# The steps of the reciprocal root: mean and intermediate value kept in PSUM beside the sums

## The chip, the cores and the metric

The kernel runs on one core of one Trainium2 chip. The metric is the device time in microseconds (us) of one execution. The median of the runs before the change is the reference point.

## The reference

Two transformer layers work on 512 tokens and 256 context tokens, both 1024 wide, in float32. In layer 0 the mixer joins a gated chunk MLP and a differential attention; in layer 1 it is a windowed attention with a sink. Each layer ends in a gated feed-forward block. What matters here is the norm that stands ahead of every block, on the attention output of each head of layer 0, and at the end:

```
def rmsnorm(x, g):
    xf = x.astype(jnp.float32)
    y = xf * lax.rsqrt(jnp.mean(xf * xf, axis=-1, keepdims=True) + EPS)
    return (y * g.astype(jnp.float32)).astype(x.dtype)
```

## The kernel before, in words

Activations lie transposed: 128 features on the partitions, tokens along the free dimension. A norm therefore needs a sum across partitions and, once the root is known, a spreading of one number per token over all partitions. Both go through TensorE.

`rstd_diag` (L145) does the first half. For each block of 128 tokens, L156 (and L161 for squares that were not added up beforehand) multiplies the squares with a matrix of ones. The result is one PSUM bank in which row p, column 128*j of a tile `ps` holds the sum of token 128*j+p; all 128 columns of a block hold the same number. VectorE (DVE) reads one column per block and turns it into mean plus epsilon: L164 in general, L166 for the heads of layer 0. That goes to a small SBUF tile `sm` of 128 x nb elements, nb being 2, 3, 4 or 6. `rsqrt_small` (L131) computes the reciprocal root from it: a first guess with integer arithmetic on the bits (L135), then three steps of three instructions each (L137, L138, L139) on SBUF tiles, ten instructions in a chain in which each needs the one before. L173 then multiplies the identity with each root, which gives nb diagonal 128 x 128 blocks, and `spread` (L183) multiplies these with ones on TensorE, which leaves the root of each token on all partitions in PSUM.

There are fourteen such chains, in order of time: the first norm of the tokens, that of the context, four heads of layer 0 (each with two sum tiles, 4 and 2 blocks), the two halves ahead of each feed-forward block (two and two), the two norms between layer 0 and layer 1, and the two halves of the final norm. A fifteenth use of `rsqrt_small`, in the chunk MLP (`rstd_small`, L125), has its input in SBUF.

The banks come from tags. `bank()` gives one of three PSUM banks (`pb` in the profile), `fill()` the only bank of its tag (`pf`), `single()` one of four (a `pw`). A bank is given out again when every instruction on its tile has ended. The heads of layer 0 take `pb` banks for their sums and for the attention itself: in `attend` (L556 on) L564 transposes exponentials into a `pb` tile, ACT and DVE split it into two SBUF tiles (L122, L123), matmuls (L106 to L108) add it into another `pb` tile, which L576 copies out.

The order of each engine's instructions is set when the program is built: a list scheduler with a model of the times takes, for each engine, the ready instruction that stands first in the program, with a few constraints written by hand (`issue_after`, `high_priority`). GpSimd (POOL) makes the low halves of the split weights (L84, L879) and some sums of squares (L791). In the last stage (`final`, L1468) it multiplies some of the output tiles (L1475), and DVE does the others (L1477).

## Time and profile before

| | |
|---|---|
| median of 3 runs | 1608.77 us (1605.66 to 1609.75) |
| the profiled execution's own time | 1603.73 us |
| its span, first to last instruction | 1601.9 us |
| mean granted TensorE clock | 0.986 |
| busy: PE / DVE / ACT / POOL | 1524.8 / 1076.4 / 722.9 / 846.9 us |

The profile is of one execution. Starts in it are microseconds from the first instruction. PE is the matmul side of TensorE, PEld its weight load. In the rows of the time-ordered view the first column is the start, the second the time to the end of the merged group, then engine, line, operation, output and inputs by the program's names, shape, and count; in brackets stands the idle time of the engine just before and what ended it.

### The profile page before, as it was taken

The numbers are of one execution on the slowest core, as the hardware profiler recorded it, in microseconds if no ns is written. First come the engines' busy times: TensorE is split into PE (matmuls) and PEld (weight loads), VectorE is DVE, ScalarE is ACT, GpSimd is POOL, SyncE is SP. The second block draws the span as 40 slices with busy tenths as digits, with TensorE's granted clock in tenths as the row PEclk, the third lists the DMA queues.
The fourth block names the chain that finished last, engine by engine and source line by source line (L and its number), as shares of the span: only waits on it lengthen the run. The fifth ranks groups of instructions, "written<-read, shape, count | busy, mean of one in ns | idle before, by whom it ended". The sixth has DMA issues, their size and how long they took to land.

```text
span 1601.9 us, 24950 instructions
## 1 busy us (share of the span) xinstructions
PE 1524.8 (95%) x9547; PEld 1354.8 (85%) x9547; DVE 1076.4 (67%) x1949; ACT 722.9 (45%) x1472; POOL 846.9 (53%) x574
## 2 busy tenths in 40 slices
PE   6999988999999999999999989999999899999996
PEld 4776877889988898999999978777869799999996
DVE  3720788765687888777676486665667966666656
ACT  2412676553542323332333244556655644444442
POOL 0463211061265767766776415541304688888883
PEclk9999999999999999999999999999999999999998
DMA  8845100033133334434442022110225133323301
GB/s 325 305 145 184 40 8 1 24 121 119 66 95 109 125 119 139 137 122 149 141 137 85 27 65 66 60 34 9 72 80 204 53 102 101 115 86 113 93 14 53
DMA packets 54295, 162.00 MB, mean 101 GB/s; under 512 B 6176, under 2 KB 10656, under 8 KB 46496
## 3 DMA queue, kind: packets, MB, share of 16 engines
q1 hardware_dynamic: 47120, 135.11, 25.3%
q10 hardware_dynamic: 7056, 25.30, 4.9%
q8 instruction: 75, 1.23, 0.3%
q14 instruction: 44, 0.36, 0.1%
HBM read 158.29 MB, written 2.10 MB: 100 GB/s over the span
## 4 chain that ended last, share of the span: by engine, by line
PE 79%; DVE 13%; ACT 3%; issue 3%; DMA 1%; POOL 0%; SPq 0%; POOLq 0%; DVEq 0%; ACTq 0%
PE pw L106 11%; PE pw L107 11%; PE pw L108 10%; PE pb L107 8%; PE pb L106 8%; PE pb L108 8%; PE pf L106 4%; PE pf L107 4%; PE pf L108 4%; DVE junk L228 3%; PE pb L1408 2%; PE pb L1397 2%; PE pf L359 2%; PE pw L1360 1%; DMA ar<-ada 1%
## 5 line engine op out<-in xcount | busy, mean ns | idle before, releaser
L84 POOL TENSOR_TENSOR w<-raw,w 128x512 fp32r<-128x512 f32 (+1 forms) x84 | 128.0, 1530 | 241.9 <-ACT w L81 219.2
L106 PE MATMUL pw<-ax,w 128*128 128x384 f32 (+2 forms) x732 | 233.9, 323 | 4.4 <-ACT ax L200 1.6
L107 PE MATMUL pw<-ax,w 128*128 128x384 f32 (+2 forms) x732 | 234.7, 321 | 2.0 <-DVE ax L466 1.4
L108 PE MATMUL pw<-ax,w 128*128 128x384 f32 (+2 forms) x732 | 233.7, 320 | 1.4 <-DVE w L944 1.4
L774 DVE SCALAR_TENSOR_TENSOR xT<-pb,mod,xT 128x512 f32<-128x512 f32 (+3 forms) x208 | 145.8, 706 | 118.2 <-PE pb L108 118.0
L879 POOL TENSOR_TENSOR w<-raw,w 128x512 fp32r<-128x512 f32 x114 | 179.6, 1590 | 39.6 <-ACT w L879 39.4
L879 POOL TENSOR_TENSOR w<-t,w 128x512 fp32r<-128x512 f32 x102 | 157.1, 1544 | 60.9 <-ACT w L879 60.9
L106 PE MATMUL pb<-hh,w 128*128 128x512 f32 x480 | 172.5, 359 | 7.8 <-DVE xT L774 5.2
L107 PE MATMUL pb<-hh,w 128*128 128x512 f32 x480 | 172.4, 359 | 3.5 <-POOL hh L123 2.8
L108 PE MATMUL pb<-hh,w 128*128 128x512 f32 x480 | 172.2, 359 | 0.0
L107 PE MATMUL pw<-T,w 128*128 128x384 f32 (+1 forms) x508 | 157.1, 310 | 1.2 <-DVE T L123 1.2
L108 PE MATMUL pw<-T,w 128*128 128x384 f32 (+1 forms) x508 | 157.1, 310 | 0.0
L106 PE MATMUL pw<-T,w 128*128 128x384 f32 (+1 forms) x508 | 156.4, 310 | 0.0
L106 PEld LDWEIGHTS pw<-ax,w 128*128 128x128 f32 x732 | 139.1, 191 | 12.9 <-ACT ax L200 2.4
L107 PEld LDWEIGHTS pw<-ax,w 128*128 128x128 f32 x732 | 139.4, 191 | 10.2 <-DVE ax L466 3.1
L106 PE MATMUL pf<-ax,w 128*128 128x256 f32 (+2 forms) x420 | 139.9, 333 | 8.3 <-DVE qf L252 5.5
L108 PEld LDWEIGHTS pw<-ax,w 128*128 128x128 f32 x732 | 139.4, 191 | 4.1 <-DVE w L944 1.7
L108 PE MATMUL pf<-ax,w 128*128 128x256 f32 (+2 forms) x420 | 138.8, 330 | 0.0
L107 PE MATMUL pf<-ax,w 128*128 128x256 f32 (+2 forms) x420 | 138.8, 330 | 0.0
L228 DVE SCALAR_TENSOR_TENSOR junk<-ar,cb 128x1024 bf16<-128x1024 f32 x64 | 111.1, 1735 | 8.7 <-DMA ar<-ada 8.1
L879 POOL TENSOR_TENSOR w<-rawo,w 128x512 fp32r<-128x512 f32 x60 | 108.9, 1816 | 11.9 <-ACT w L879 11.9
L879 DVE TENSOR_TENSOR hs<-hs,pw 128x384 f32<-128x384 f32 (+1 forms) x114 | 55.2, 484 | 87.3 <-PE pw L108 74.8
(377 smaller groups left out, 3938.0 us busy)
## 6 DMA issues: line engine op xcount, KB each, us to landing
raw<-ffn_in SPq DMA_DIRECT2D x44, 1024.0 KB, 5.0
ar<-ada SPq DMA_DIRECT2D x24, 1024.0 KB, 7.0
ar<-ada ACTq DMA_DIRECT2D x48, 512.0 KB, 3.5
rawo<-ffn_out SPq DMA_DIRECT2D x88, 256.0 KB, 3.0
raw<-odd_out SPq DMA_DIRECT2D x32, 256.0 KB, 2.7
raw<-qk SPq DMA_DIRECT2D x16, 256.0 KB, 7.8
raw<-uv SPq DMA_DIRECT2D x16, 256.0 KB, 2.7
raw<-even_out SPq DMA_DIRECT2D x8, 512.0 KB, 3.5
```

The costliest lines, as they stand in the source:

```text
L84: eng.tensor_tensor(lo, raw, hi.bitcast(F32), ALU.subtract)
L106: mm(out, s[0], m[0], start=start, stop=False, **kw)
L107: mm(out, s[0], m[1], start=False, stop=False, **kw)
L108: return mm(out, s[1], m[0], start=False, stop=stop, **kw)
L228: return self.nc.vector.scalar_tensor_tensor(junk, t, 1.0, self.cb[who], ALU.mult, ALU.mult, accum_out=self.acc[who][:, col:col + 1])
L359: nc.tensor.matmul(ps[32 * q:32 * q + 32, :w], cst[:, k, :], t[:, w * q:w * q + w], start=k == 0, stop=k == KT - 1, skip_group_check=True)
L774: ins = self.nc.vector.scalar_tensor_tensor(h, ps[:, r], self.modcol(l, j, m, who), h, ALU.mult, ALU.add)
L879: tail[key] = fn(*args, **kw)
L1360: nc.tensor.matmul(ps[:, st:en], Q, K[g][p][:, b0 * P:b1 * P], start=p == 0, stop=p == 1, skip_group_check=True)
L1397: last = nc.tensor.transpose(pt[:, x * P:(x + 1) * P], es[2 * (x % 2) + x // 2][:, kb * P:(kb + 1) * P], self.ident)
L1408: nc.tensor.matmul(po[64 * h:64 * h + 64, :], V[vb][:, 64 * g:64 * g + 64], t[:, h * TC:h * TC + TC], start=kb == 0, stop=kb == nb - 1, sk ...
```

## The change

A new function `rsqrt_room` takes the mean `v` and a place `t` for the intermediate value from outside. `rstd_diag` passes both as columns of the first sum tile: columns 1 to nb for the mean, columns 33 to 32+nb for the intermediate value. Column 0 of each block still holds the sum that is read, and the other columns of the bank held copies that nobody reads. Only the root `y` is a small SBUF tile, as before. The products are grouped differently, so that each instruction takes one operand from PSUM and one from SBUF: before, y times y times v; now, v times y times y. The number of instructions is the same. `rsqrt_small` stays for the chunk MLP.

```
+    def rsqrt_room(self, v, n, t):
+
+        ve = self.nc.vector
+        y = self.small(n)
+        ve.tensor_scalar(y.bitcast(I32), v.bitcast(I32), -0.5, float(0x5F3759DF), ALU.mult, ALU.add)
+        for _ in range(3):
+            ve.tensor_tensor(t, v, y, ALU.mult)
+            ve.scalar_tensor_tensor(t, t, -0.5, y, ALU.mult, ALU.mult)
+            ve.scalar_tensor_tensor(y, t, 1.5, y, ALU.add, ALU.mult)
+        return y
...
-        ms = self.small(nb)
+        ms, room = None, None
...
             col = ps[:, 0:T].rearrange("p (j f) -> p j f", f=P)[:, :, 0]
+            if ms is None:
+                ms, room = ps[:, 1:1 + nb], ps[:, 33:33 + nb]
...
-        r = self.rsqrt_small(ms, nb)
+        r = self.rsqrt_room(ms, nb, room)
```

## The prediction

> **What bounds the kernel now.** I read the busy times first, then the chain of work that ended last, then the fourteen chains by a table over stretches, then the time order where one of them is stretched.

> ```profile
> PE 1524.8 (95%) x9547; PEld 1354.8 (85%) x9547; DVE 1076.4 (67%) x1949; ACT 722.9 (45%) x1472; POOL 846.9 (53%) x574
> ```

> ```profile
> PE 79%; DVE 13%; ACT 3%; issue 3%; DMA 1%; POOL 0%; SPq 0%; POOLq 0%; DVEq 0%; ACTq 0%
> ```

> PE bounds the whole; DVE (VectorE) holds 13% of the chain that ended last. A change on DVE counts only in those places. The next table takes, for some stretches that each hold one chain without its diagonal, the small tiles alone: the stretch, its length, DVE's busy time on them, and the count.

> ```profile
> 14.00:16.24 2.24, 1.80 (x11) 0.00 (x0) 1.00 1.03 410
> 45.70:54.24 8.54, 4.82 (x11) 0.00 (x0) 1.00 1.03 419
> 226.20:238.51 12.31, 1.91 (x12) 0.00 (x0) 0.86 0.00 0
> 268.60:279.46 10.86, 1.83 (x12) 0.00 (x0) 1.00 0.01 2
> 411.50:414.90 3.40, 2.99 (x11) 0.00 (x0) 1.00 0.55 188
> 1234.50:1237.25 2.75, 2.40 (x10) 0.00 (x0) 1.00 0.70 221
> 1583.70:1587.31 3.61, 2.32 (x11) 0.00 (x0) 1.00 0.02 5
> ```

> Undisturbed, eleven instructions take 1.80 us of a stretch of 2.24: 0.164 us each, one every 0.20. The second row is 3.02 above that, the last three 1.19, 0.76 (ten instructions) and 0.52 us. The two heads (12 instructions each) are not stretched, only drawn out by other work between the steps. What stretches a step shows between the layers:

> ```profile
> 949.73 2.61 POOL L84 TENSOR_TENSOR w<-raw,w 128x512 fp32r<-128x512 f32 x2 [4.04 <-ACT w L81]
> ```

> ```profile
> 949.89 1.23 DVE L137 TENSOR_TENSOR sm<-sm 128x2 f32<-128x2 f32 x1
> 951.05 0.74 DVE L199 SCALAR_TENSOR_TENSOR t<-xT,mod,pf 128x512 f32<-128x512 f32 x1
> 951.71 0.65 DVE L138 SCALAR_TENSOR_TENSOR sm<-sm,sm 128x2 f32<-128x2 f32 x1
> 952.28 0.74 DVE L201 SCALAR_TENSOR_TENSOR ax<-t,mod,ax 128x512 fp32r<-128x512 f32 x1
> ```

> POOL (GpSimd) works from 949.73 to 952.34, two instructions of 1.3 us. L137, both inputs in SBUF, takes 1.23 us and ends with the first of them; L138 takes 0.65 and ends with the second. L199, which reads PSUM and one SBUF tensor, runs beside the second from 951.05 in 0.74 us, no longer than L201 takes after POOL has ended. So the stall belongs to two SBUF inputs beside a working POOL, and the change takes it from all nine steps of a chain. The biggest case is the last chain:

> ```profile
> 1589.04 4.12 POOL L1475 TENSOR_TENSOR xT<-xT,rs 128x256 f32<-128x256 f32 x6 [3.68 <-ACT rs L1465]
> 1589.79 0.68 DVE L138 SCALAR_TENSOR_TENSOR sm<-sm,sm 128x2 f32<-128x2 f32 x1
> ...
> 1593.22 0.48 DVE L173 TENSOR_SCALAR dg<-ident,sm 128x128 f32<-128x128 f32 x2
> ...
> 1593.76 1.22 PE L183 MATMUL pf<-dg,ones 128*128 128x256 f32 x2 [5.20 <-DVE dg L173]
> 1595.07 0.37 ACT L1465 COPY rs<-pf 128x256 f32<-128x256 f32 x1 [6.10 <-PE pf L183]
> ...
> 1595.52 2.09 POOL L1475 TENSOR_TENSOR xT<-xT,rs 128x256 f32<-128x256 f32 x3 [2.35 <-ACT rs L1465]
> ```

> PE idles 5.20 us for this diagonal, ACT 6.10 for PE, POOL 2.35 for ACT. Nothing covers the chain; it is the end of the kernel.

> **The change part by part.** *The last chain.* Its last five steps lie from 1589.79 to 1593.22, 3.43 us. At one every 0.20 they take 1.0, and the diagonal could start 2.4 us earlier, at 1590.8. But there POOL is still at its six multiplications (until 1593.16), and the diagonal, with input and output in SBUF, can wait for POOL too:

> ```profile
> 944.42 1.26 POOL L84 TENSOR_TENSOR w<-raw,w 128x512 fp32r<-128x512 f32 x1 [6.73 <-ACT w L81]
> 944.48 1.88 DVE L173 TENSOR_SCALAR q<-ident,sm 128x128 f32<-128x128 f32 x4
> ```

> Four diagonals took 1.88 us there, where twice 0.48 would do. At the end each of the two diagonals can be held until an instruction of POOL ends (4.12/6 = 0.69 us each, half of it on the mean), which gives back up to 0.9 in all. Gain 1.5 to 2.4; I take 1.9, the middle. The chain before it loses its 0.52 too, but PE's sums for the last chain don't come earlier by that; what little it brings is inside the 1.9.

> *Between the layers.* L137 and L138 lose 1.23 + 0.65 - 2 x 0.16 = 1.56 us. But L201 has two SBUF inputs and would now arrive at about 951.1, just as POOL's second instruction has started: it would wait to 952.34, run 0.74, and end near 953.0, as it does now. The stall only changes its instruction. Bounds 0 and 1.56; I take 0.3, nearer to what the rows give.

> *The covered chains* (3.02, 1.19, 0.76). What PE waits for in them:

> ```profile
> PE pw L107 <- DVE ax L466: 1.4, 2, 0.8
> ```

> ```profile
>   PE pf L183: 6.6, 2
> ...
>   PE pb L183: 1.3, 2
> ```

> The first row is of the waits from 40 to 62: PE waited 1.4 us for products that DVE had queued around the second row's chain. The other two list who waited for the small tiles' chains in the whole run: PE's spreading four times, 5.20 of the 6.6 in the last chain. So at 411 and 1234 the diagonal was there before PE came to it, and 1.19 and 0.76 are worth nothing as long as PE's order has dense matmuls ahead of L183; without that cover they would count as they stand. Around 46 to 54 the bounds are 0 and 1.4; I take 0, since the small chain is only a part of what lay ahead of those products.

> *Each instruction by itself.* PSUM as an input is in the trace; PSUM as DVE's output is not.

> ```profile
> L138 DVE SCALAR_TENSOR_TENSOR sm<-sm,sm x42: 147/161/1245, 14.7 to 1591.9; 128x2 f32<-128x2 f32 x18, 128x6 f32<-128x6 f32 x12, 128x4 f32<-128x4 f32 x6, 128x3 f32<-128x3 f32 x6
> ...
> L166 DVE SCALAR_TENSOR_TENSOR sm<-pb,sx x8: 124/156/161, 226.3 to 319.8; 128x4 f32<-128x4 f32 x4, 128x2 f32<-128x2 f32 x4
> ```

> Minimum, median and maximum in ns: 156 with a PSUM input, 161 without. A PSUM input costs nothing. For the output I take the same, the nearest row; the spread of L166 (124 to 161) bounds it at about 0.04 us either way. It counts in four chains, the last two and the two between the layers: 44 instructions, 1.8 us either way. [...]

> *The bank.* This is the wait that the change adds. The first sum tile stays in use until the chain's last step. In `pf` and `pw` nobody wants the bank before the spreading. For the heads it is one of three `pb`, now free after one read at the start of the two long stretches of the table, then held for all of their 12.31 and 10.86 us if DVE's order stays. In them lie:

> ```profile
> 232.58 1.05 PE L564 MATMUL pb<-ident,e 128*128 128x128 f32 x4
> ...
> 233.00 0.68 DVE L123 TENSOR_TENSOR atl<-pb,ath 128x512 fp32r<-128x512 f32 x1
> ```

> ```profile
> 272.83 0.60 PE L564 MATMUL pb<-ident,e 128*128 128x128 f32 x4
> ...
> 274.12 0.68 DVE L123 TENSOR_TENSOR atl<-pb,ath 128x512 fp32r<-128x512 f32 x1
> ```

> One of the other two banks is the attention's sum, so the second block's transposes (L564) must wait until DVE has split the first (L123), to 233.68 and 274.80: 1.1 and 2.0 us. Behind them on PE stand the next scores, and for those wait DVE's maxima and ACT's exponentials.

> ```profile
> 226.00:281.00 55.00, 44.32 (x257) 37.71 (x256) 46.43 (x135) 38.14 (x75) 7.43 (x5) 0.91 0.00 1
> ```

> In these 55 us PE is busy for 44.32 and DVE for 46.43, so with 8.6 idle on the fullest engine most of 3.1 can be caught up. Bounds 0 and 3.1; I take 0.8, a quarter. The third head's chain is short, and the fourth has no attention behind it.

> **Sum** against the profiled execution: -1.9 - 0.3 + 0 + 0.8 = -1.4 us, from 1603.73 to 1602.3 (its span is 1601.9, and the 1.8 around it don't change). The profiled execution lies 5.0 us under the median of the runs; the forecast for the median is 1608.77 - 1.4 = 1607.4 us.

> **The rivals.** *The bank serializes the attention* (slower). If the steps stay as far apart as now, each further block of transposes in the hold has to wait for the split of the one before: transposes 0.60, DVE 0.68 and ACT's part, some 2 us. With two late blocks at each of two heads that is 8 us, less 1.9 at the end: +6, or 1615. It decides itself at whether the chain still runs when the second block is due; today it does, by 5.9 and 6.6 us. Against it: PE has other work ready, and nothing but the interleaving keeps a chain from its 2.24 us.

> *All stalls come back* (faster). If the covered 3.02 and the 1.56 lie on the path as well, the gain is 1.9 + 3.0 + 1.6 - 0.8 = 5.7: 1603.1. For it: DVE is in the chain in both places. Against it: the waits of only 1.4 us and the collision at 951.1.

> *Writing PSUM is slower*: at 0.04 us for 44 instructions the sum is +0.4, 1609.2.

> *The stalls stay*, because the one SBUF input that is left meets POOL as well: the change doesn't do what it can, and the bank's 0.8 remains, 1609.6. Against it stands L199 at 951.05.

> **How the numbers follow.** The forecast has 0.48, with a range of its own from -5 to +2; the bank 0.22; all stalls back 0.14; slower writes 0.09; stalls that stay 0.07. About 0.3% (4.8 us) is what a measurement of this kernel tells from no change. Faster by more: nearly all of "all stalls back" and a small part of the forecast, 0.17. Slower: the bank near its price, and the tails of the others where the scheduler's order shifts, 0.20. Within: 0.63. For 8 in 10 the range reaches from "all stalls back" with 2 us more to the bank's price: 1601 to 1615.

> **What would show it.** Right: no step above 0.2 us beside a working POOL; PE's idle time ahead of the last L183 down from 5.20 to about 3.3; L201 stalled near 951. The bank: a longer time from 226 to 281, with PE idle ahead of L564. Wrong: steps above 0.2 us without POOL beside them (slow PSUM writes), steps of 0.65 beside L1475 (stalls that stay), or another order of the heads that moves more than all these terms.

## The result and the profile after

The changed kernel takes 1610.11 us (median of 22 runs, 1605.64 to 1612.6). The kernel before, run beside it on the same chip, takes 1605.8 (22 runs, 1604.1 to 1609.75). The ratio is 1.0021, with a 95% interval from 1.0014 to 1.0028: slower by 2.2 to 4.5 us, where a gain of 1.4 was forecast. The time lies in the range and within 0.3%, but on the other side of no change.

The profiled execution of the changed kernel has a span of 1607.9 us (1601.9 before) and a granted clock of 0.980 (0.986). From its page, the busy times and the chain that ended last:

```profile
PE 1531.2 (95%) x9547; PEld 1362.0 (85%) x9547; DVE 1070.4 (67%) x1949; ACT 723.0 (45%) x1472; POOL 847.3 (53%) x574
...
PE 78%; DVE 13%; ACT 3%; issue 2%; DMA 2%; POOL 1%; SPq 0%; POOLq 0%; DVEq 0%; ACTq 0%
```

DVE works 6.0 us less, as the change means it to: no instruction of the steps is stalled any more (the longest takes 0.17 us). PE works 6.4 us more at the same number of matmuls. So the loss does not look like an added wait on PE. It looks like longer matmuls.

To find the place, I set the starts of equal matmuls in the two traces against each other. Up to 225 us the changed kernel runs 1.2 us ahead, from 325 on 4.9 behind, at the end 6.0 behind. The lead of 1.2 is not to be credited to the change: at 200 us the other kernels tried below lie anywhere from 0.5 ahead of the kernel before to 1.3 behind it. Behind that point lie three gains or losses: 6.0 lost between 225 and 325, beside the heads of layer 0; 2.3 lost between 1172 and 1216; 1.8 won in the last stage.

The first place in a table over stretches. The stretches end where both kernels have done the same part of the matmul work, so rows of one rank can be compared. Columns: stretch, length, busy time of PE, PEld, DVE, ACT and POOL with counts, granted clock, share and rate of the DMA engines. First before, then after:

```profile
224.94:244.94 20.00, 12.78 (x70) 9.95 (x69) 17.73 (x48) 17.82 (x32) 3.09 (x2) 0.85 0.00 0
244.94:271.94 27.00, 24.50 (x151) 21.82 (x150) 20.89 (x58) 17.53 (x38) 3.56 (x3) 0.92 0.00 1
271.94:291.91 19.97, 19.01 (x116) 16.64 (x117) 17.33 (x49) 9.78 (x22) 1.03 (x1) 1.00 0.00 1
291.91:323.54 31.63, 30.48 (x195) 26.16 (x194) 24.22 (x101) 20.41 (x44) 0.00 (x0) 1.00 0.18 63
sum 98.60, PE 86.77 PEld 74.57 DVE 80.18 ACT 65.54 POOL 7.68; mean PE 21.69 PEld 18.64 DVE 20.04 ACT 16.38 POOL 1.92
```

```profile
223.77:246.11 22.34, 14.26 (x71) 12.04 (x70) 19.16 (x57) 19.00 (x34) 3.10 (x2) 0.72 0.00 0
246.11:269.73 23.62, 23.15 (x151) 20.27 (x149) 17.20 (x45) 14.04 (x32) 2.56 (x2) 0.98 0.00 1
269.73:291.85 22.12, 20.55 (x119) 17.91 (x119) 19.27 (x49) 11.03 (x24) 2.12 (x1) 0.92 0.01 1
291.85:328.37 36.52, 32.53 (x194) 27.80 (x193) 25.25 (x103) 21.31 (x48) 0.00 (x0) 0.95 0.16 54
sum 104.60, PE 90.49 PEld 78.03 DVE 80.88 ACT 65.38 POOL 7.77; mean PE 22.62 PEld 19.51 DVE 20.22 ACT 16.34 POOL 1.94
```

The same work takes 104.60 us instead of 98.60. Of these 6.0 us, 3.7 are longer matmuls (PE's sum 86.77 to 90.49) at a lower clock, and 2.3 are idle time of PE (11.83 to 14.11). It is not lost in one place: the first row loses 2.3, the second wins 3.4, the third and fourth lose 2.1 and 4.9. In the timed runs of the changed kernel, too, the time goes with the granted clock: the two at 0.988 take 1605.6 and 1606.1 us, the four at 0.986 1608.2 to 1608.5, the nine at 0.980 1609.7 to 1612.6.

How it begins is told by ACT's time order, before and then after:

```profile
233.67 0.59 ACT L122 CAST ath<-pb 128x512 fp32r<-128x512 f32 x1
...
234.74 1.28 ACT L632 ACT_TABLE_LOAD   x1
236.03 3.04 ACT L632 ACTIVATE f<-f 128x768 f32<-128x768 f32 x4
```

```profile
233.53 1.28 ACT L645 ACT_TABLE_LOAD   x1
...
242.38 0.58 ACT L122 CAST ath<-pb 128x512 fp32r<-128x512 f32 x1
```

L122 copies the transposes of a block of exponentials out of their `pb` bank. Before, the second block's copy (233.67) goes ahead of the table load for the GELUs. After, it comes only at 242.38, behind the GELUs, the next table load and the next exponentials. Why, PE's time order of the changed kernel shows:

```profile
232.56 0.79 PE L555 MATMUL pw<-kh,qa 128*128 128x512 f32 x1 [0.96 <-ACT e L559]
...
234.86 0.41 PE L108 MATMUL pb<-ath,vlo 128*128 128x256 f32 x1
235.08 1.05 PE L577 MATMUL pb<-ident,e 128*128 128x128 f32 x4
...
242.53 0.80 PE L555 MATMUL pw<-kh,qa 128*128 128x512 f32 x1 [4.43 <-ACT e L559]
```

The transposes L577 (L564 before) start at 235.08. Before, they start at 232.58, which is 231.4 on the clock of the changed kernel, and there the scores (L542) come behind them. Now the next scores (L555) and the first block's products (L107, L108) stand ahead of them, and they are 3.7 us late. No idle time stands in front of them; 0.96 us stand ahead of the scores at 232.56, where the transposes were before, and the profile puts these down to an exponential. So the bank that is held does not show as a wait of the transposes: the program was built in another order around it, since the third bank of the tag is held and the transposes need the one that L123 must split first.

By then ACT's place for the copy has passed, and PE idles 4.43 us for exponentials. But this idle time is not the loss: the second row of the table repays it, because PE then works 23.15 of 23.62 us. The first two stretches together take 1.0 us less than before. The loss is what comes after, in the third and fourth, where the attention's order is another one as well. It is not for want of dense matmuls to put beside the attention: the tile `ax` alone (the chunk MLP's dense matmuls) in the fourth stretch, before and after, has the same count, and so it has in the three others (0, 48 and 48).

```profile
291.91:323.54 31.63, 15.47 (x71) 11.78 (x72) 0.00 (x0) 0.00 (x0) 0.00 (x0) 1.00 0.18 63
```

```profile
291.85:328.37 36.52, 14.93 (x71) 11.66 (x72) 0.00 (x0) 0.00 (x0) 0.00 (x0) 0.95 0.16 54
```

In that stretch PE waits for a split of the transposes by DVE, goes on slowly, and later waits for a copy by ACT:

```profile
298.20 0.50 PE L107 MATMUL pb<-atl,vhi 128*128 128x256 f32 x1 [1.41 <-DVE atl L123]
298.50 0.41 PE L108 MATMUL pb<-ath,vlo 128*128 128x256 f32 x1
...
299.56 1.91 PE L167 MATMUL pb<-ones,sq 128*128 128x128 f32 x8
...
312.30 0.39 PE L106 MATMUL pf<-ax,w 128*128 128x256 f32 x1 [1.34 <-ACT f L598]
```

A matmul of 256 columns takes 0.41 us where it takes 0.28 elsewhere in that head, and the eight sums of the next chain take 1.91 us where the kernel before has 1.06. In the kernel before PE has no idle time above 0.2 us in this stretch but 0.73 and 0.22 near its end, and the changed kernel has these two as well.

### The profile page after: what moved, and what is told of

Its sections match the earlier page's. It is cut to its first block, busy times and chain, and to the rows that moved or that the text cites. A ratio compares the mean times of both kernels' runs of the same rounds, so it can differ in the third digit from the quotient of the medians.

```text
span 1607.9 us, 24953 instructions
## 1 busy us (share of the span) xinstructions
PE 1531.2 (95%) x9547; PEld 1362.0 (85%) x9547; DVE 1070.4 (67%) x1949; ACT 723.0 (45%) x1472; POOL 847.3 (53%) x574
## 3 DMA queue, kind: packets, MB, share of 16 engines
q8 instruction: 75, 1.23, 0.3%
## 4 chain that ended last, share of the span: by engine, by line
PE 78%; DVE 13%; ACT 3%; issue 2%; DMA 2%; POOL 1%; SPq 0%; POOLq 0%; DVEq 0%; ACTq 0%
PE pw L106 10%; PE pw L108 10%; PE pw L107 10%; PE pb L107 8%; PE pb L106 8%; PE pb L108 8%; PE pf L106 4%; PE pf L107 4%; PE pf L108 4%; DVE junk L241 3%; PE pb L1421 2%; PE pb L1410 2%; PE pf L372 2%; PE pw L1373 1%; DMA ar<-ada 1%
## 5 line engine op out<-in xcount | busy, mean ns | idle before, releaser
L84 POOL TENSOR_TENSOR w<-raw,w 128x512 fp32r<-128x512 f32 (+1 forms) x84 | 128.5, 1537 | 240.8 <-ACT w L81 216.5
L107 PE MATMUL pw<-ax,w 128*128 128x384 f32 (+2 forms) x732 | 235.2, 322 | 1.5 <-DVE ax L479 1.4
L108 PE MATMUL pw<-ax,w 128*128 128x384 f32 (+2 forms) x732 | 234.9, 322 | 1.4 <-DVE w L957 1.4
L107 PE MATMUL pb<-hh,w 128*128 128x512 f32 x480 | 172.5, 359 | 3.7 <-POOL hh L123 2.8
L108 PE MATMUL pb<-hh,w 128*128 128x512 f32 x480 | 172.4, 359 | 0.0
L107 PE MATMUL pw<-T,w 128*128 128x384 f32 (+1 forms) x508 | 157.1, 310 | 1.2 <-DVE T L123 1.2
L108 PE MATMUL pw<-T,w 128*128 128x384 f32 (+1 forms) x508 | 157.0, 310 | 0.0
L107 PEld LDWEIGHTS pw<-ax,w 128*128 128x128 f32 x732 | 140.6, 192 | 8.8 <-DVE ax L479 2.2
L108 PEld LDWEIGHTS pw<-ax,w 128*128 128x128 f32 x732 | 140.5, 192 | 4.4 <-DVE w L957 1.7
L108 PE MATMUL pf<-ax,w 128*128 128x256 f32 (+2 forms) x420 | 138.7, 330 | 0.0
L107 PE MATMUL pf<-ax,w 128*128 128x256 f32 (+2 forms) x420 | 138.5, 330 | 0.0
```

Of the source, the lines that this page charges most:

```text
L84: eng.tensor_tensor(lo, raw, hi.bitcast(F32), ALU.subtract)
L107: mm(out, s[0], m[1], start=False, stop=False, **kw)
L108: return mm(out, s[1], m[0], start=False, stop=stop, **kw)
```

## The experiments

The theory: the loss comes from the **hold of the heads' first sum bank**, and the rest of the change wins a little. The rivals: steps that write PSUM are slower by themselves; another order in layer 1, where the chain near 1171 is spread late; or chance of the clock. All ratios are to the kernel before on the same chip.

**PSUM everywhere but in the heads.**

```
-        ms, room = None, None
+        psum = eps is None
+        ms, room = (None, None) if psum else (self.small(nb), None)
...
-        r = self.rsqrt_room(ms, nb, room)
+        r = self.rsqrt_room(ms, nb, room) if psum else self.rsqrt_small(ms, nb)
```

> The change everywhere but at the four heads of layer 0, whose steps stay in SBUF. Theory A (the heads' sum bank, held through the chain, delays the attention): the lag of 6 us that the changed kernel gathers between 220 and 310 us is gone, the 1.9 us at the end stay won, the 2.3 us lost at the chain near 1171 stay lost; in sum within 1 us of the kernel before. Theory B (each step on PSUM is dearer, wherever it is): most of the loss stays, 3 us slower than before.

Measured: 1605.01 against 1606.15 us, ratio 0.999 (0.9981 to 0.9999). Ten of the fourteen chains in PSUM are worth 0.2 to 3.0 us.

**PSUM in the heads alone**: the same edit with `psum = eps is not None`.

> The change at the four heads alone. Theory A: the whole lag of 6 us between 220 and 310 us is there, and nothing is won at the end: 4 to 6 us slower than before, slower than the changed kernel. Theory B: forty of the 140 steps, so no more than a third of the loss, 1 us.

Measured: 1610.87 against 1606.15 us, ratio 1.0032 (1.002 to 1.0044). The heads lose 3.2 to 7.1 us. The two halves add up: 1.0032 and 0.999 make 1.0022, and the whole change measures 1.0021. The first and the last of the four stretches of this kernel, and their sum:

```profile
225.98:248.33 22.35, 14.24 (x72) 12.02 (x71) 19.15 (x57) 19.00 (x34) 3.09 (x2) 0.72 0.00 0
...
294.02:330.58 36.56, 32.56 (x194) 27.82 (x193) 25.23 (x104) 21.32 (x48) 0.00 (x0) 0.95 0.15 53
sum 104.60, PE 90.44 PEld 77.93 DVE 80.83 ACT 65.35 POOL 7.75; mean PE 22.61 PEld 19.48 DVE 20.21 ACT 16.34 POOL 1.94
```

All four stretches are as long as those of the changed kernel to 0.05 us, in another kernel and on another execution. So this is a different course of the work and not a chance of one run.

**Only the hold.** The kernel before, and of the heads' steps only the third one's intermediate value goes to the first sum bank; the mean and the rest stay in SBUF.

```
-        for _ in range(3):
+        for i in range(3):
+            t = last if i == 2 and last is not None else t
...
-        r = self.rsqrt_small(ms, nb)
+        r = self.rsqrt_small(ms, nb, last=ps0[:, 33:33 + nb] if eps is not None else None)
```

> The kernel before, with one thing from the change: at the four heads the third step's intermediate value lies in the first sum bank, so that the bank is held as long as in the changed kernel, while seven of the ten instructions stay in SBUF and nothing else differs. Theory A: the same lag as with the heads alone in PSUM, 4 to 6 us slower than before. Theory B or a theory of the instruction order by modelled step times: less than a third of it, 1 us or less.

Measured: 1610.18 against 1606.15 us, ratio 1.0028 (1.0017 to 1.0039). With nearly all steps in SBUF, the loss of the heads is there in full. Of its table the last row and the sum:

```profile
292.96:329.49 36.53, 32.55 (x194) 27.78 (x193) 25.25 (x103) 21.31 (x48) 0.00 (x0) 0.95 0.16 54
sum 104.70, PE 90.50 PEld 78.01 DVE 80.98 ACT 65.36 POOL 7.89; mean PE 22.63 PEld 19.50 DVE 20.25 ACT 16.34 POOL 1.97
```

So it is not the speed of the steps. What is left is the hold to the end of the chain, or that any step touches the bank at all; the next run tells these two apart.

**A shorter hold.** The same with the first step's intermediate value (`i == 0`).

> The kernel before, with the first step's intermediate value (not the third's) of the four heads in the first sum bank: as many instructions on PSUM as in the kernel that held the bank to the third step, but the bank comes free after the fourth instruction of the chain. Theory A (the length of the hold decides): less than half of that kernel's 4 us of loss; at the first head the bank is free at about 233, when the second block of transposes was due at 232.6, so its copy by ScalarE stays ahead of the GELUs. Rival: any touch of PSUM between the steps turns the planned order and costs the same 4 us.

Measured: 1605.44 against 1605.7 us, ratio 1.0004 (0.9993 to 1.0015): as many instructions on PSUM as in the kernel above, but not its loss (the two intervals don't overlap). The interval leaves up to 2.4 us open, and the runs are spread: six of eleven take 1603.3 to 1605.4 us, five 1608.1 to 1610.1, the profiled one among these, while of the 27 before two lie above 1608. PE in time order shows that the transposes do wait for the step:

```profile
232.95 1.12 PE L577 MATMUL pb<-ident,e 128*128 128x128 f32 x4 [0.37 <-DVE sm L140]
```

They are some 0.5 us late (before's 232.58 is 232.4 on this clock). The copy comes between the GELUs instead of behind them, and the attention is not thrown back: the first, second and fourth stretch take 0.30, 0.45 and 0.06 us less than before. So the fourth, in which the changed kernel loses most, is whole again. What counts is thus the length of the hold, and not that a step touches the bank. The third takes 2.9 more, 2.7 of them in longer matmuls at a clock of 0.85:

```profile
270.99:293.90 22.91, 21.71 (x116) 18.66 (x117) 17.23 (x49) 9.78 (x22) 1.04 (x1) 0.85 0.00 1
```

The kernel with SBUF heads lost 1.6 in that stretch by its clock alone, with the idle time of before:

```profile
272.34:293.89 21.55, 20.58 (x117) 17.88 (x117) 17.35 (x49) 9.80 (x22) 1.04 (x1) 0.92 0.00 1
```

So at least a part of the 2.9 needs no hold; whether all of it does without, and whether it makes the five longer runs, isn't shown. Of the two lengths tried, the hold that makes the transposes 0.5 us late costs nothing in the median, and the one that makes them 3.7 us late costs 3 to 7.

**The last two chains alone**: the first edit with `psum = at is not None`.

> The change at the two chains of the final norm alone, where the bank is one of four that nobody else wants. All theories that take the stall beside GpSimd for real: 1.5 to 2.5 us faster than before, PE's idle time ahead of the last spreading down from 5.2 to about 3.4 us. If the time between the layers or the chain near 1171 moved anything else in the changed kernel, it is not here. Theory B: no faster than before.

Measured: 1604.32 against 1606.15 us, ratio 0.9991 (0.9983 to 1.0). In its trace PE's wait ahead of the last spreading is 3.39 us, as in the changed kernel, and the last stage wins 1.8. This kernel also shows the clock by itself. Here is a stretch in layer 1 in which its order is that of before, with the same stretch of the kernel described last:

```profile
1212.00:1217.00 5.00, 5.00 (x32) 5.00 (x31) 5.00 (x5) 2.70 (x6) 5.00 (x4) 0.66 0.36 107
```

```profile
1212.00:1217.00 5.00, 5.00 (x44) 5.00 (x43) 5.00 (x5) 2.36 (x6) 5.00 (x4) 1.00 0.30 101
```

PE is busy throughout in both, and does 32 matmuls in the one and 44 in the other. The lower clock costs 1.4 to 1.5 us of the run, by an estimate from such counts (12 matmuls of 44 here, 13 in the kernel described next), and it is there in four of the nine profiles (the changed kernel's among them), with the order of before in two of these.

**Only the intermediate value in PSUM**, in the last two chains; mean in SBUF, products grouped as before.

```
+            t = last if last is not None else t
...
-        r = self.rsqrt_small(ms, nb)
+        r = self.rsqrt_small(ms, nb, last=ps0[:, 33:33 + nb] if at is not None else None)
```

> The kernel before, with only the intermediate value of the last two chains in the sum bank and the mean in SBUF, products grouped as before. The first instruction of each step then reads the root twice from SBUF and writes PSUM; the second and third read one operand from each. If two SBUF inputs are what waits for GpSimd, the first instruction of a step beside GpSimd's multiplications takes 0.65 us and the other two 0.16, and about 1.2 of the 1.9 us are won. If an SBUF output is what waits, the third instruction of each step is the slow one. If any access to SBUF waits, all three stay at 0.65 us.

Measured: 1605.0 against 1605.7 us, ratio 0.9995 (0.9986 to 1.0004); in the trace the last stage wins 1.8, as much as with both values in PSUM. POOL and DVE in the last chain, two views of this kernel:

```profile
1591.33 4.14 POOL L1488 TENSOR_TENSOR xT<-xT,rs 128x256 f32<-128x256 f32 x6 [3.66 <-ACT rs L1478]
```

```profile
1592.27 0.16 DVE L140 SCALAR_TENSOR_TENSOR sm<-pw,sm 128x2 f32<-128x2 f32 x1
1592.46 0.30 DVE L138 TENSOR_TENSOR pw<-sm 128x2 f32<-128x2 f32 x1
1592.80 0.17 DVE L139 SCALAR_TENSOR_TENSOR pw<-pw,sm 128x2 f32<-128x2 f32 x1
```

With one input from SBUF and one from PSUM a step takes 0.16 to 0.17 us beside POOL, whether it writes PSUM or SBUF; so beside an input from PSUM neither one SBUF input nor an SBUF output was enough for a stall. The instruction that reads the root twice from SBUF takes 0.30. POOL's six instructions take 0.69 each, so the second ends at 1592.71, and this one at 1592.76: that fits a wait for the end of POOL's instruction. Less is given up than was expected, since only one such instruction met POOL. That the same tile read twice counts as two inputs is left likely, not shown. Two inputs are not needed for every stall, though: the first guess of the chain before (L135), with one input and its output both in SBUF, takes 0.59 us beside POOL's sums (three from 1585.29, 2.38 us in all), where it takes 0.17 in the last chain; in the kernel before it takes 1.07 at 1234.71, beside POOL's work from 1232.77 to 1235.76. So the forecast's "two SBUF inputs" is too narrow.

**All but the heads and the chain near 1171.** The first edit with `psum = eps is None and not (bank == self.fill and accs[0][1] == 256)`.

> The change without the four heads and without the chain of layer 1 near 1171 (both with steps in SBUF). If the order that moved at 1171 costs what the traces suggest (0.6 to 1 us), this is 2 us faster than before and up to 1 us faster than the kernel that only left out the heads; if that place cost nothing and the differences between the traces there were a clock's, the two are the same within their intervals.

Measured: 1602.96 against 1605.7 us, ratio 0.9982 (0.9973 to 0.999): 1.6 to 4.3 us faster than before, and so faster than the changed kernel as well. Its heads take as long as before's, and the last stage wins 2.05:

```profile
sum 98.32, PE 88.18 PEld 75.81 DVE 80.46 ACT 65.54 POOL 7.76; mean PE 22.04 PEld 18.95 DVE 20.11 ACT 16.38 POOL 1.94
```

Why that chain was left out: in the changed kernel a maximum of the attention (L1384, 0.82 us long) went ahead of its diagonal, as DVE's time order shows.

```profile
1179.25 0.16 DVE L150 SCALAR_TENSOR_TENSOR sm<-pf,sm 128x2 f32<-128x2 f32 x1
...
1179.45 0.82 DVE L1384 TENSOR_REDUCE sa<-pw 128x1 f32<-128x640 f32 x1
1180.18 0.47 DVE L186 TENSOR_SCALAR q<-ident,sm 128x128 f32<-128x128 f32 x2
```

Before, the diagonal goes ahead of that maximum. In the two kernels that have this chain in PSUM in the same way (the changed one and the one with SBUF heads), the matmuls fall back by 0.55 us between 1174 and 1186; in the six others, by nothing. Most of the rest of the 2.3 us lost there, 1.4, is the clock near 1212, as above. That these 0.55 us are worth something in the times isn't shown: 0.9982 and 0.999 have intervals that overlap.

## Why the prediction was wrong

**The step that failed is the bank**: "Bounds 0 and 3.1; I take 0.8, a quarter", and ahead of it "with 8.6 idle on the fullest engine most of 3.1 can be caught up". It measured 6.0 us in the profile, and 3.2 to 7.1 by the runs of the heads alone: above the upper bound. The rest of the sum, a gain of 2.2, lies within the 0.2 to 3.0 that the kernel with SBUF heads won. Among the signs of being wrong the prediction has what came, "another order of the heads that moves more than all these terms", but the sum has no price for it; the sign for the bank, PE idle ahead of the transposes, isn't in the trace. Three things were left out of the bound.

- It priced the transposes at the wait for L123, 1.1 and 2.0 us. But the built order put other work ahead of them, and nothing was reckoned for what stands behind them on ACT. In ACT's order as it was built, the late copy lost its place to 1.28 us of table load, 3 us of GELUs and more. The view that tells it is ACT's time order of before: the copy starts at 233.67 and the table load at 234.74. There was 1.1 us of room at most for a delay of 3.7, and the shorter hold, 0.5 us late, missed the place as well.
- Its window ended at 281 us. The catching up did happen, 3.4 us in the second stretch, and with it the late copy at the first head was paid back. But the order of the attention behind it had changed too, and the third head, whose share was put at nothing ("The third head's chain is short"), lost 4.9 us in its stretch: 2.8 idle, 1.41 and 1.34 of them in two waits that the kernel before doesn't have, and 2.1 in longer matmuls. No run holds the bank at one head alone, so which head's hold gives that stretch its order stays open.
- It reckoned with idle time alone. Of 6.0 us, 3.7 were slower matmuls: six pieces at half the clock lie in these stretches, three before (the last section has what such a piece is).

The argument that the chain could close up ("nothing but the interleaving keeps a chain from its 2.24 us") did not help: at the first head it ran from 225.10 to 235.64, 10.5 us instead of 12.3, still drawn out by the other work of DVE.

The sum had no term either for the 2.3 us lost in layer 1, 0.55 by another order and 1.4 by one piece at half the clock.

**The rival of the bank** had the size: it gave +6 against the profiled execution, with two late blocks at two heads at 2 us each, less the last chain. The profiles differ by 6.0, but with 6.0 lost at the heads, 2.3 in layer 1 and 1.8 won at the end: that the sums agree is in part luck. Its point of decision was right (the chain still runs when the second block is due), its working only in part: the first head pays at once and gets it back, and the third head's stretch, which it left out, pays the most.

**Right: the last chain.** 1.9 us were forecast and 1.8 measured. The diagonals are held up beside POOL, as forecast (it works from 1596.92 to 1601.06); the last stage of the changed kernel, DVE and PE's waits:

```profile
1598.26 0.17 DVE L149 SCALAR_TENSOR_TENSOR pw<-pw,sm 128x2 f32<-128x2 f32 x1
1598.46 0.16 DVE L150 SCALAR_TENSOR_TENSOR sm<-pw,sm 128x2 f32<-128x2 f32 x1
1598.65 1.12 DVE L186 TENSOR_SCALAR dg<-ident,sm 128x128 f32<-128x128 f32 x2
```

```profile
PE pf L196 <- DVE dg L186: 3.4, 1, 3.4
```

The steps come one every 0.20, the two diagonals take 1.12 instead of 0.48 (0.48 also in the chain before them, at 1595.20, with POOL idle), and PE idles 3.4 us instead of 5.20.

**Right: the stall between the layers changes its instruction.** DVE in the changed kernel there:

```profile
955.93 0.83 DVE L214 SCALAR_TENSOR_TENSOR ax<-t,mod,ax 128x512 fp32r<-128x512 f32 x1
...
956.76 1.69 DVE L214 SCALAR_TENSOR_TENSOR ax<-t,mod,ax 128x512 fp32r<-128x512 f32 x1
```

The steps are quick there (0.15 to 0.16 us each), and L214 (L201 before), with two SBUF inputs, takes 1.69 us. POOL works there from 954.83 to 959.60; the L214 ahead of that, which starts beside POOL as well, takes 0.83, and the one at 960.46, behind POOL's end, 0.74. Of the 0.3 us taken for it nothing shows.

**Right: the covered chains are worth nothing**, though their stalls go. The small tiles alone in the changed kernel, two of the stretches:

```profile
44.50:53.60 9.10, 2.62 (x12) 0.00 (x0) 1.00 1.03 420
...
416.40:419.50 3.10, 2.34 (x13) 0.00 (x0) 1.00 0.39 148
```

The first was 4.82 for eleven instructions. The matmuls behind the first place come 0.2 us earlier, those behind the second not at all.

**Right: a write to PSUM costs next to nothing.** All the steps of one line in the changed kernel (minimum, median, maximum in ns), with a `pb` bank as the output and then SBUF:

```profile
L149 DVE SCALAR_TENSOR_TENSOR pb<-pb,sm x27: 154/168/173, 14.5 to 1243.9; 128x6 f32<-128x6 f32 x12, 128x2 f32<-128x2 f32 x9, 128x4 f32<-128x4 f32 x3, 128x3 f32<-128x3 f32 x3
L150 DVE SCALAR_TENSOR_TENSOR sm<-pb,sm x27: 147/161/166, 14.7 to 1244.1; 128x6 f32<-128x6 f32 x12, 128x2 f32<-128x2 f32 x9, 128x4 f32<-128x4 f32 x3, 128x3 f32<-128x3 f32 x3
```

7 ns more for the output; for the input nothing, as the median of 161 is that of the steps with SBUF alone (L138 of the kernel before).

**The base.** The forecast of 1607.4 us started from a median of three runs, 1608.77. With 22 runs beside the changed kernel the median before is 1605.8, so the forecast came near the measured 1610.11 for a reason that has nothing to do with its steps. The ratio is what counts, and there it was on the wrong side.

## What to carry to other kernels

Scratch values in a bank of PSUM cost next to nothing as instructions (7 ns here), but they hold the bank: look at who takes the next bank of the same tag, and follow the late instruction through the queues behind it. A table load or a long group ahead of which it loses its place is where the delay jumps (here 1.28 and 3.05 us), the builder's order may show no wait of the late instruction at all, and the loss may come a whole head later. Where a bank is in short supply, hold it to the first step or not at all; where nobody wants it, as in the last chains, moving one of two inputs from SBUF to PSUM took the stall beside POOL from the steps (0.65 to 0.68 us each before, 0.16 to 0.17 after), up to the next instruction that works on SBUF alone (the two diagonals, 1.12 us instead of 0.48). And price a slip not only in idle time: the clock can cost more (1.6 us alone, with the idle time of before, in the third stretch of the kernel with SBUF heads) when PE is busy for about half of a piece of 3.41 us, or for less (1.76 us ahead of the fall at 298.32).

## What the hardware showed unexpectedly

```profile
294.91:298.32 3.41, 1.76 (x9) 0.90 (x8) 3.41 (x13) 2.88 (x7) 0.00 (x0) 1.00 0.03 5
298.32:301.73 3.41, 3.41 (x17) 3.41 (x18) 1.89 (x11) 0.75 (x4) 0.00 (x0) 0.50 0.00 0
```

In all nine traces the clock is either full or half (1.00 or 0.50), and between its changes lie whole multiples of 3.413 us. A piece at half clock costs up to 1.7 us where PE works throughout, by an estimate (half of 3.41). I divided each trace from about 18 us on into pieces on the grid of its own changes, and counted. Of the pieces at full clock, 68 had PE busy for less than 0.45 of their length, and half clock followed all of them; of 45 between 0.45 and 0.60 it followed 27; of 3927 at 0.60 or more, none. Of the pieces at half clock, full clock followed all 86 with PE busy for 0.90 or more and none of the 49 below that. In the traces of before and of the changed kernel alone these counts are 15 of 15, 7 of 8, none of 874, 20 of 20 and none of 9. (The ends of matmuls are modelled, so these shares are rough.) The length of a single idle time doesn't decide: in the changed kernel half clock followed the piece at 267.60, with 1.93 us busy and no idle time in it above 1.01, and in the kernel before full clock followed the piece at 269.77, with 1.76 busy and an idle time of 1.66.

This fits that kernels of one order had the loss near 1212 and had it not. Each idles 1.6 us there for weights. In three traces an edge of the grid parts this idle time, the two pieces are busy for 0.67 to 0.85 each, and the clock stays full (before: 2.87 and 2.30 of 3.41 us, on both sides of 1208.43). In the six others it lies in one piece, which is left 0.52 to 0.53 busy, and four of these fell to half clock (the changed kernel: 1.79 of 3.42 us, from 1213.09). Where the grid lies against the work differs from trace to trace, so that a part of what the profile of one execution shows is chance.
